# Three buffers for the tile that holds S1 and S3, and longer planned transfers, in the FFN schedule of a two-layer encoder trunk

## The chip, the cores and the metric

The kernel runs on one core of a Trainium2 chip. The metric is the device time of one execution in microseconds; a time is the median of several executions. Before the change it is 1542.79 us, the median of three runs (1539.48 to 1547.44).

## What is computed

The input is one sequence of 512 tokens of width 1024 and a memory of 256 tokens, all float32. Two layers follow one another. Each has a mixer (layer 0: forgetting and differential attention, layer 1: an mLSTM), a cross-attention to the memory, and a gated FFN with a causal convolution. Every part starts with an RMS norm and is added to the residual stream. The change touches the FFN alone:

```python
def conv_ffn(xn, w_up, conv_w, conv_b, w_down):
    h = causal_depthwise_conv(xn @ w_up, conv_w) + conv_b
    g, u = jnp.split(h, 2, axis=-1)
    return (jax.nn.gelu(g) * u) @ w_down
...
        x = x + conv_ffn(rms_norm(x, ffn_norm[layer]), ffn_w_up[layer], ffn_conv_w[layer],
                         ffn_conv_b[layer], ffn_w_down[layer])
```

`w_up` is 1024 x 5632 (2816 columns of g, 2816 of u), `w_down` is 2816 x 1024, and the convolution has three taps.

## The kernel before

**Precision.** The activations stand transposed, with the 1024 features on partitions in 8 blocks of 128 and the 512 tokens along the free dimension. Every product is done in three matmuls: each operand is split into a rounded high part (`wh`, `xh`) and the rest (`wl`, `xl`), and `mm3` (lines 268 to 270) adds high x high, high x low and low x high. A weight therefore goes through four steps before TensorE can use it: a DMA from HBM, a cast on ScalarE that makes the high part, a subtraction on VectorE that makes the low part (line 259), and the matmuls.

**Pairs.** The FFN works through 22 pairs p: block p of 128 columns of g and block p of 128 columns of u. Seven of them go through `plain`, which does the product directly. The 15 pairs in `SEVEN` (4 to 15 and 17 to 19) go through `seven`, which does the 2 x 2 block product in the seven products of Strassen's method in Winograd's form: the blocks are the two column blocks (g and u), the two halves of the 1024 features, and the two halves of 256 tokens. A1 is the weight block of g, A2 that of u, each 128 x 1024 in SBUF, whose first 512 columns belong to the first four feature blocks. The combinations of the activations (T1 to T4) are formed once in a layer by `forms` (lines 1230 to 1243, and 259), four times with k = 0 to 3, through a tile `sa` each time.

**The combinations of the weights are made by DMA.** For a pair the queue of SyncE loads, at line 1152, the first halves of A1 and A2 into a tile `sa` of 1024 columns (512 KB); GpSimd (POOL) then issues a DMA that adds A2 onto it (`b1`, line 1319). `sa` now holds S3 in its first half and S1 in its second, and `w1` splits it for p5 and p7. In the same way SyncE loads the first half of A1 into `sb` (256 KB), POOL adds the second half of `sa` onto it (`b2`: the tile is S2, split by `w2` for p6), and when that split is done, adds the second half of A1 (`b4`: the tile is S4, split by `w4` for p3). p1 and p2 take A1 itself (`raw`, split by `w3`), p4 takes the second half of A2 (`ra`, split by `w22`). The texts below write "sa load", "sa sum", "sb load", "S2 sum" and "S4 sum" for these five transfers, with the pair in brackets, s2h(5) and s2l(5) for the cast and the subtraction of `w2` of pair 5, and w1h, w1l, s4h, s4l, a22h likewise. The casts of `seven` are at line 1337, those of whole blocks at 1166.

**The products and their sums.** p1 and p2 add into one accumulator, and ScalarE writes -p1 to `v` in between (line 1373), so that p2 waits for `v`. p6, p7 and p4 add into a second one; VectorE reads it into `u2` ahead of p7 and into `u3` ahead of p4. p5 and p3 share a third one, and `c22` is read ahead of p3. `u2`, `u3`, `c22`, `c21` and `c12` are all at line 1378. There is one buffer of `v`, of `s2`, of `s4` and of `a22`. At line 1399 a pair's result is scaled; `tail` then does the convolution (ScalarE line 1257, VectorE line 1264), the gelu (1272), the product with u (1274) and the split of the result (1278 and 259).

**What fills the gaps.** From pair 5 on, `fill` puts blocks of the down projection (`down`; in the profile w<-ah,wh) between the products of a pair. Their weights come through a tile `dr` of two buffers.

**The order.** `Sched` plans every engine's order. Each piece of work is a task with an engine, a duration, the tasks it depends on, a due time and the buffers it takes and frees. A buffer is taken in the order in which the tasks were made, and a task on another engine may start `lat` after the end of what it depends on:

```python
                    for d in t.deps:
...
                        at = max(at, d.end + (0.0 if d.eng == e else d.lat))
...
                    for r, _ in t.take:
                        if want[r][0] is not t:
                            ok = False
                            break
                        at = max(at, self.slots[r][self.slot(r)])
```

At each step the task that can start first is written to the program. The framework that builds the program takes this order as a priority and sets the final order of each engine's queue by itself, so that the two differ in places. In the chip each queue then runs in order, and an instruction waits until its operands are there. The times that the plan assumes are not seen by the chip; only the order and the number of buffers are.

In the plan a load (`load`) lasts 0.0017 us a column, and a sum (`onto`) 0.0029 us a column, on their queues; what depends on them may start 2.0 and 2.5 us after that. `raw` has 3 buffers, `dr`, `sa`, `sb` and `ra` have 2 each. Buffers are used in turn.

Of the kernel before, what the change touches and what calls it, by code (L numbers as in the profile page):

```python
# [13 lines left out]
ALU = mybir.AluOpType  # L14
# [45 lines left out]
class Plan:  # L60
# [11 lines left out]
    def add(self, fn, dur=0.0, deps=(), prio=None, take=(), free=(), chain=(), pre=(), after=0.0, order=(), load=(), st=None):  # L72
        it = Item(fn, dur, [d for d in deps if d is not None], len(self.items) if prio is None else prio, take, free, chain, pre, after, order, load, st)
        it.n = len(self.items)
        self.items.append(it)
        return it
# [141 lines left out]
class Builder:  # L218
# [22 lines left out]
    def bank(self, tag):  # L241
        tag, bufs = BANKS[tag]
        return self.til(self.aux, tag, bufs=bufs)
# [875 lines left out]
    def ffn_steps(self, layer, mp):  # L1119
# [1 line left out]


        nc, t = self.nc, self.t
        sc = Sched(raw=3, h=3, s2=1, s4=1, a22=1, sa=2, sb=2, ra=2, hs=2, c=1, dr=2, v=1, u2=1, u3=1, act=10, acc=4, s=2, w=2)
        add = sc.add
        tt = lambda n: 0.14 + 1.06e-3 * n
        act = lambda n: 0.2 + 0.83e-3 * n
# [11 lines left out]
        def joined(deps, prio, free):  # L1139
            return add("-", 0.0, None, deps, prio, (), free, 0.0)  # L1140

        RAWS = {"raw": (self.wp, 1024, 3), "dr": (mp, 512, 2), "sa": (mp, 1024, 2), "sb": (mp, 512, 2), "ra": (mp, 512, 2)}

        def raw_tile(st, tag):
            pool, n, bufs = RAWS[tag]
            st[tag] = self.til(pool, tag, (P, n), bufs=bufs)
            return st[tag]

        def load(st, tag, src, cols, at):
            def fn():  # L1150
                to = raw_tile(st, tag)[:, :cols]
                nc.sync.dma_start(to.rearrange("p (a b) -> p a b", a=2) if len(src.shape) == 3 else to, src)

            return add("SP", 0.0017 * cols, fn, (), at, [(tag, st)], (), 2.0)

        def parts(st):
            st["wh"], st["wl"] = (self.til(self.wp, n, (P, 1024), F32R, bufs=3) for n in ("wh", "wl"))
# [1 line left out]
        def weight(src, cols, at, tag="raw"):  # L1159

            st = {}
            l = load(st, tag, src, cols, at - 9.0)

            def hi():
                parts(st)
                nc.scalar.copy(st["wh"][:, :cols], st[tag][:, :cols])

            h = add("ACT", act(cols), hi, [l], at - 3.0, [("h", st)])
            lo = add("DVE", tt(cols), lambda: self.sub(st["wl"][:, :cols], st[tag][:, :cols], st["wh"][:, :cols]), [h], at - 2.0, (), [(tag, st)])
            return st, lo  # L1170
# [139 lines left out]
        def seven(p, fill):  # L1310
            st, sa, sb, r2, f1, f3, s2, s4, a22 = ({} for _ in range(9))
            at = clock[0]
# [3 lines left out]


            def onto(out, src, cols, deps, due):
                return add("POOL", 0.0029 * cols, lambda: nc.gpsimd.dma_start(out(), src(), accum_op=ALU.add), deps, due, (), (), 2.5)

            SB = lambda: sb["sb"][:]
            b1 = load(sa, "sa", up2[p][:, :, :512], 1024, at - 20.0)
            b1 = onto(lambda: sa["sa"][:], lambda: A2, 1024, [b1], at - 16.0)
            b2 = load(sb, "sb", A1[:, :512], 512, at - 18.0)
            b2 = onto(SB, lambda: sa["sa"][:, 512:], 512, [b1, b2], at - 9.0)
            l2 = load(r2, "raw", A1, 1024, at - 10.0)
            l1 = load(a22, "ra", A2[:, 512:], 512, at - 6.0)
# [15 lines left out]
            w2 = split(s2, 512, [b2], at, lambda: small(s2, "s2"), [("s2", s2)], SB)  # L1343
            w1 = split(f1, 1024, [b1], at + 1.0, lambda: parts(f1), [("h", f1)], lambda: sa["sa"][:])
            b4 = onto(SB, lambda: A1[:, 512:], 512, [w2], at - 1.5)
            w22 = split(a22, 512, [l1], at + 4.0, lambda: small(a22, "a22"), [("a22", a22)], lambda: a22["ra"][:], [("ra", a22)])
            w4 = split(s4, 512, [b4], at + 5.0, lambda: small(s4, "s4"), [("s4", s4)], SB, [("sb", sb)])
# [27 lines left out]
            def sum_(tag, out, a, b, op):  # L1375
                if tag:
                    st[tag] = self.til(mp, tag, (P, 256), bufs=1)
                tt_(out=out(), in0=a(), in1=b(), op=op)
# [3 lines left out]
            hs = lambda j, l: (lambda: st["hs_"][:, j, 2 + 256 * l : 258 + 256 * l])  # L1382
            v = add("ACT", act(256), v_, [p1], at + 1.5, [("v", bv)])
            u2 = add("DVE", 0.42, lambda: sum_("u2", tmp("u2"), bank("Y"), tmp("v_"), ALU.add), [p6, v], at + 4.0, [("u2", bu2)])
# [4 lines left out]
            u3 = add("DVE", 0.42, lambda: sum_("u3", tmp("u3"), bank("Y"), tmp("v_"), ALU.add), [p7], clock[0], [("u3", bu3)])  # L1389
# [38 lines left out]
        due = {4 * c + 5 + c // 3: c for c in range(4)}  # L1428
# [384 lines left out]
```

## Time and profile before

| what | value |
|---|---|
| median of three runs | 1542.79 us (1539.48 to 1547.44) |
| the profiled execution | 1540.91 us |
| its span, first to last instruction | 1539.1 us |
| mean granted clock of TensorE | 0.990 |
| busy: TensorE, VectorE, ScalarE, POOL | 98%, 75%, 52%, 8% |
| FFN of layer 0, its Strassen pairs | about 462 to 716 us |
| FFN of layer 1, its Strassen pairs | about 1203 to 1463 us |
| DMA: from the hardware queues, from POOL's | 159.8 MB, 31.5 MB |
| share of the 16 DMA engines' span | 31.4%, 12.2% |

How rows are read. A timeline row has the start in us from the span's start, the duration, the engine, the line, the operation with out<-in, and in square brackets how long the engine was idle before it and what ended that. A row of the waits has the total, how many times, and the longest. A row of the windows has the stretch, its length, the busy time and the number of instructions (x) of TensorE's matmuls, its weight loads, VectorE, ScalarE and POOL, then the granted clock of TensorE, the mean busy share of the 16 DMA engines, and GB/s. A group row ends in busy time, mean ns of one, and idle time before it. DMA rows give the KB of one and the median us from issue to landing. In the chain of waits a row has the start, the length and what lasted that long; for a DMA that is from issue to landing. Names stand without buffer numbers; the pair of an instruction follows from its place among those of its line.

### The profile page before, as it was taken

How to read it: one execution, taken by the hardware profiler on the slowest of the kernel's cores; microseconds unless marked ns; L12 is line 12 of the kernel's file. 1: busy time of each engine (PE TensorE's matmuls, PEld its weight loads, DVE VectorE, ACT ScalarE, POOL GpSimd, SP SyncE). 2: the span in 40 equal slices, each digit the busy share in tenths (PEclk: the TensorE clock that was granted, in tenths of full speed). 3: DMA queues.
4: the chain of work that ended last, by engine and by line, in shares of the span. 5: the costliest groups of instructions: out<-in, count | busy, mean ns of one | idle time of the engine just before them, and what ended most of it. 6: DMA issues, size and time to landing. Idle time of an engine off the chain costs nothing. (4 is left out here: it accounts for less than half of the span.)

```text
span 1539.1 us, 22626 instructions
## 1 busy us (share of the span) xinstructions
PE 1501.5 (98%) x8458; PEld 1301.7 (85%) x8458; DVE 1156.7 (75%) x2167; ACT 798.6 (52%) x1342; POOL 117.3 (8%) x168
## 2 busy tenths in 40 slices
PE   9999999999998999999999999999999898989998
PEld 8888888888888988998887778888888798989987
DVE  7889875665787877888678866676658687888874
ACT  6767564443555544554446544344446454455544
POOL 2000120000001111110001000000000211111000
PEclk9999999999999999999999999999999999999999
DMA  5222232332448867752222222232324887776422
GB/s 176 83 69 83 83 125 96 110 110 69 144 143 196 207 168 196 202 149 86 86 96 82 89 77 96 96 117 76 123 83 142 187 201 188 200 172 177 114 66 76
DMA packets 72926, 193.80 MB, mean 126 GB/s; under 512 B 8048, under 2 KB 8048, under 8 KB 72816
## 3 DMA queue, kind: packets, MB, share of 16 engines
q1 hardware_dynamic: 58848, 159.77, 31.4%
q0 software_dynamic: 12960, 31.46, 12.2%
q8 instruction: 66, 1.08, 0.3%
q10 hardware_dynamic: 1008, 1.12, 0.2%
q14 instruction: 44, 0.36, 0.1%
HBM read 182.36 MB, written 2.10 MB: 120 GB/s over the span
## 5 line engine op out<-in xcount | busy, mean ns | idle before, releaser
L268 PE MATMUL acc<-xh,wh 128*128 128x512 f32 (+1 forms) x848 | 311.5, 367 | 14.9 <-ACT v L1373 14.9
L270 PE MATMUL acc<-xh,wl 128*128 128x512 f32 (+1 forms) x848 | 306.7, 362 | 0.0
L269 PE MATMUL acc<-xl,wh 128*128 128x512 f32 (+1 forms) x848 | 306.5, 361 | 0.0
L259 DVE TENSOR_TENSOR wl<-raw,wh 128x1024 fp32r<-128x1024 f32 (+2 forms) x203 | 243.6, 1200 | 42.7 <-ACT wh L262 38.1
L262 ACT CAST wh<-raw 128x1024 fp32r<-128x1024 f32 (+2 forms) x137 | 140.9, 1030 | 168.5 <-PE acc L269 99.7
L268 PEld LDWEIGHTS acc<-xh,wh 128*128 128x128 f32 x848 | 161.2, 190 | 39.4 <-ACT v L1373 16.1
L270 PEld LDWEIGHTS acc<-xh,wl 128*128 128x128 f32 x848 | 161.4, 190 | 24.1
L269 PEld LDWEIGHTS acc<-xl,wh 128*128 128x128 f32 x848 | 161.5, 190 | 23.2
L1264 DVE SCALAR_TENSOR_TENSOR c<-hs,vec,c 128x512 f32<-128x512 f32 x176 | 127.0, 747 | 11.3 <-ACT c L1257 10.7
L268 PE MATMUL w<-ah,wh 128*128 128x512 f32 x304 | 119.4, 393 | 0.0
L269 PE MATMUL w<-al,wh 128*128 128x512 f32 x304 | 119.2, 392 | 0.0
L270 PE MATMUL w<-ah,wl 128*128 128x512 f32 x304 | 118.3, 389 | 0.0
L1257 ACT ACTIVATE c<-hs,vec 128x512 f32<-128x512 f32 x88 | 69.1, 811 | 45.7 <-DVE hs L1399 39.5
L495 DVE TENSOR_TENSOR x<-w,x 128x512 f32<-128x512 f32 x72 | 49.5, 687 | 26.1 <-PE w L270 26.1
L270 PEld LDWEIGHTS w<-ah,wl 128*128 128x128 f32 x304 | 57.4, 189 | 12.3
L268 PEld LDWEIGHTS w<-ah,wh 128*128 128x128 f32 x304 | 57.6, 190 | 10.2
L269 PEld LDWEIGHTS w<-al,wh 128*128 128x128 f32 x304 | 57.6, 189 | 9.8
L330 PE MATMUL acc<-wl,xh 128*128 128x256 f32 (+1 forms) x192 | 61.9, 323 | 0.2 <-DVE wl L259 0.2
L329 PE MATMUL acc<-wh,xh 128*128 128x256 f32 (+1 forms) x192 | 61.7, 326 | 0.0
L331 PE MATMUL acc<-wh,xl 128*128 128x256 f32 (+1 forms) x192 | 61.7, 322 | 0.0
L268 PE MATMUL acc<-mem,wh 128*128 128x256 f32 (+1 forms) x192 | 61.5, 320 | 0.0
L269 PE MATMUL acc<-mem,wh 128*128 128x256 f32 (+1 forms) x192 | 61.1, 318 | 0.0
(373 smaller groups left out, 3742.1 us busy)
## 6 DMA issues: line engine op xcount, KB each, us to landing
raw<-in_up_dram SPq DMA_DIRECT2D x58, 512.0 KB, 4.5
dr<-in_down_dram SPq DMA_DIRECT2D x64, 256.0 KB, 3.3
sa<-in_up_dram SPq DMA_DIRECT2D x30, 512.0 KB, 4.7
sa<-in_up_dram POOLq DMA_DIRECT2D x30, 512.0 KB, 5.7
raw<-in_xk_dram SPq DMA_DIRECT2D x16, 512.0 KB, 3.2
raw<-in_wo_dram SPq DMA_DIRECT2D x16, 512.0 KB, 3.3
raw<-in_xq_dram SPq DMA_DIRECT2D x16, 512.0 KB, 3.2
raw<-in_xv_dram SPq DMA_DIRECT2D x16, 512.0 KB, 3.2
```

What stands on the lines that cost most here:

```text
L259: self.nc.vector.tensor_tensor(out=lo, in0=v, in1=hi.bitcast(F32), op=ALU.subtract)
L262: self.nc.scalar.copy(hi, v)
L268: mm(out, wh, xh, start=first, stop=False, skip_group_check=parts)
L269: mm(out, wh, xl, start=False, stop=False, skip_group_check=parts)
L270: mm(out, wl, xh, start=False, stop=last, skip_group_check=parts)
L329: mm(ps, xh[k][:, ts], wh[:, ws], start=(k == 0), stop=False)
L330: mm(ps, xh[k][:, ts], wl[:, ws], start=False, stop=False)
L331: mm(ps, xl[k][:, ts], wh[:, ws], start=False, stop=(k == 7))
L495: self.nc.vector.tensor_tensor(out=self.x[m][:], in0=ps[:], in1=self.x[m][:], op=ALU.add)
L1257: nc.scalar.activation(st["c_"][:, j, :], hs()[:, j, 2:514], AF.Identity, scale=self.col("cw", (layer * 3 + 2) * 44 + blk), bias=self.col( ...
L1264: nc.vector.scalar_tensor_tensor(out=c, in0=hs()[:, j, n : n + 512], scalar=w, in1=c, op0=ALU.mult, op1=ALU.add)
```

## The change

```diff
-        sc = Sched(raw=3, h=3, s2=1, s4=1, a22=1, sa=2, sb=2, ra=2, hs=2, c=1, dr=2, v=1, u2=1, u3=1, act=10, acc=4, s=2, w=2)
+        sc = Sched(raw=3, h=3, s2=1, s4=1, a22=1, sa=3, sb=2, ra=2, hs=2, c=1, dr=2, v=1, u2=1, u3=1, act=10, acc=4, s=2, w=2)
...
-        RAWS = {"raw": (self.wp, 1024, 3), "dr": (mp, 512, 2), "sa": (mp, 1024, 2), "sb": (mp, 512, 2), "ra": (mp, 512, 2)}
+        RAWS = {"raw": (self.wp, 1024, 3), "dr": (mp, 512, 2), "sa": (mp, 1024, 3), "sb": (mp, 512, 2), "ra": (mp, 512, 2)}
...
-            return add("SP", 0.0017 * cols, fn, (), at, [(tag, st)], (), 2.0)
+            return add("SP", 0.0017 * cols, fn, (), at, [(tag, st)], (), 4.0)
...
-                return add("POOL", 0.0029 * cols, lambda: nc.gpsimd.dma_start(out(), src(), accum_op=ALU.add), deps, due, (), (), 2.5)
+                return add("POOL", 0.0029 * cols, lambda: nc.gpsimd.dma_start(out(), src(), accum_op=ALU.add), deps, due, (), (), 6.0)
```

The tile `sa` gets a third buffer, in the plan and in SBUF (4 KB more on each partition). The delay that the plan adds to a load grows from 2.0 to 4.0 us, and that of a sum from 2.5 to 6.0 us. No instruction is added or removed: in the built program every engine has the same work in another order, and the waits for a slot of `sa` refer to the tile three before instead of two before. In SBUF the tiles behind `sa` move up by 4 KB.

The order moves as follows, alike in both layers. On SyncE and POOL the sa load and the sa sum of a pair stand one pair earlier among the others. On ScalarE, VectorE and TensorE the order changes around pairs 4 to 6, and in single places at pairs 9 and 10, and 13 and 14. Pieces of the built orders, before and after (cv, gelu, ah and al are steps of `tail`, dr and drl the splits of a down block, a number behind them its count):

```text
POOL    before: sa(4) S2(4) sa(5) S4(4) S2(5) sa(6) S2(6) S4(5) sa(7) S4(6) S2(7) sa(8)
        after:  sa(4) sa(5) S2(4) S2(5) sa(6) S4(4) sa(7) S4(5) sa(8) S2(6) S4(6) S2(7)
        before: S2(9) S4(8) sa(10) S2(10) S4(9) S4(10) sa(11) S2(11)
        after:  S2(9) S4(8) sa(11) S2(10) S4(9) S4(10) sa(12) S2(11)
ScalarE before: v(4) cv3 s4h(4) s2h(5) gelu3 w1h(5) c11(4) ah3 dr0 a22h(5) v(5) s4h(5) s2h(6) cv4 cv4 dr1
        after:  v(4) cv3 s4h(4) w1h(5) c11(4) gelu3 s2h(5) ah3 dr0 a22h(5) v(5) s2h(6) s4h(5) dr1
        both:   dr8 ah7 s2h(10) a22h(9) v(9) s4h(9)
VectorE before: tap3 tap3 u2(4) tap3 s4l(4) tap3 s2l(5) u(3) w1l(5) u3(4) drl0 ... c12(4) scaling(4) u2(5) s4l(5) s2l(6)
        after:  tap3 x4 w1l(5) u(3) u2(4) s2l(5) al3 s4l(4) u3(4) ... c12(4) s2l(6) scaling(4) s4l(5) u2(5)
TensorE before: p1(4) p6(4) p5(4) p2(4) p7(4) p1(5) p5(5) p4(4) p3(4) p6(5) p2(5) down p7(5)
        after:  p1(4) p5(4) p2(4) p6(4) p1(5) p7(4) p6(5) p4(4) p5(5) p3(4) p2(5) down p7(5)
        before: p1(9) p6(9) p4(8) p3(8) p5(9) p2(9)
        after:  p1(9) p6(9) p5(9) p4(8) p3(8) p2(9)
```

In the new TensorE order p2(4) stands in the middle of p5(4).

## The prediction

> **What bounds the kernel now.** I read first the page: TensorE is busy for 98% of the span, so only its idle time and a slower clock can be won back. Then the waits of TensorE, then each long one in its timeline.
>
> ```profile
> PE 1501.5 (98%) x8458; PEld 1301.7 (85%) x8458; DVE 1156.7 (75%) x2167; ACT 798.6 (52%) x1342; POOL 117.3 (8%) x168
> ...
> PE acc L268 <- ACT v L1373: 14.9, 5, 4.8
> ```
>
> ```profile
> 475.14 0.58 PE L268 MATMUL s<-th,wh 128*128 128x256 f32 x1 [4.50 <-ACT wh L1337]
> 549.20 0.58 PE L268 MATMUL acc<-xh,wh 128*128 128x256 f32 x1 [3.46 <-ACT v L1373]
> 615.01 0.39 PE L268 MATMUL acc<-xh,wh 128*128 128x256 f32 x1 [1.99 <-ACT v L1373]
> 1217.94 0.38 PE L268 MATMUL s<-th,wh 128*128 128x256 f32 x1 [4.60 <-ACT wh L1337]
> 1293.40 0.58 PE L268 MATMUL acc<-xh,wh 128*128 128x256 f32 x1 [4.79 <-ACT v L1373]
> 1361.40 0.46 PE L268 MATMUL acc<-xh,wh 128*128 128x256 f32 x1 [4.48 <-ACT v L1373]
> ```
>
> The six long waits lie in the two FFNs. Four are p2 of pairs 9 and 13 (of each layer) waiting for `v`; two are p5 of pair 5, at the start of the Strassen pairs, waiting for `w1`. The windows behind them show a second price:
>
> ```profile
> 474.10:480.90 6.80, 5.29 (x23) 5.00 (x24) 3.94 (x7) 2.30 (x5) 1.74 (x2) 0.50 0.84 178
> 549.20:552.60 3.40, 3.40 (x14) 3.30 (x15) 3.37 (x7) 2.20 (x4) 1.30 (x2) 0.50 0.62 116
> 612.80:618.00 5.20, 3.21 (x21) 2.75 (x21) 4.14 (x8) 3.12 (x6) 1.75 (x2) 1.00 0.92 217
> 1293.30:1296.70 3.40, 3.30 (x14) 3.20 (x15) 3.36 (x6) 2.04 (x5) 1.41 (x2) 0.50 0.62 106
> 1361.50:1365.00 3.50, 3.50 (x15) 3.31 (x16) 3.46 (x7) 2.14 (x4) 1.34 (x2) 0.51 0.61 118
> ```
>
> After an idle time of 3.46 us or more the granted clock is 0.50 for 3.4 us (6.8 us behind the 4.50), which loses half of it; after 1.99 us it stays 1.00.
>
> The Trainium skill ("TensorE: Matmul & The Clock Gate", Part 1) says that the clock halves after an idle window of about 3.4 us and returns after a busy one. The trace agrees: 3.46 us of idle cost 3.40 us at 0.50, and 1.99 us cost none. By that rule a wait that shrinks below some 3 us loses its second price too.
>
> **Why `v` is late: the third buffer's part.** On ScalarE's queue the cast of the S2 sum of pair 10 stands ahead of pair 9's `a22` cast and its `v`, and the built program keeps it there (s2h(10), a22h(9), v(9)) before and after the change: so the longer planned transfer doesn't reorder this. What it waits for is a sum:
>
> ```profile
> 533.10 0.33 SPq L1152 DMA_DIRECT2D sb<-in_up_dram  x1
> 534.43 0.86 POOL L1319 DMA_DIRECT2D sa<-in_up_dram  x1 [8.88 <-DVE hs L1399]
> 540.55 0.86 POOL L1319 DMA_DIRECT2D sb<-sa  x1 [5.25 <-DMA sa<-in_up_dram]
> 547.05 0.62 ACT L1337 CAST s2h<-sb 128x512 fp32r<-128x512 f32 x1 [6.97 <-DMA sb<-sa]
> 548.76 0.38 ACT L1373 ACTIVATE v<-acc 128x256 f32<-128x256 f32 x1 [0.57 <-DVE hs L1378]
> ```
>
> The S2 sum of pair 10 (540.55) waited for the sa sum of the same pair (534.43), which could not be loaded before a slot of two came free. With three slots that place in both queues belongs to pair 11, and pair 10's sa sum is done a pair earlier. Then the S2 sum waits only for its sb load and for POOL to issue pair 11's sa sum.
>
> ```profile
> sb<-in_up_dram SPq DMA_DIRECT2D x30, 256.0 KB, 4.0
> sb<-sa POOLq DMA_DIRECT2D x30, 256.0 KB, 4.3
> DMA to landing us min/median/max: 2.5/4.6/9.0
> ```
>
> Load at 533.10 + 4.0 = 537.1, issue at about 537.7; the sum takes its median 4.3 to the 6.4 of now (540.55 to the cast at 547.05): it lands at 542.0 to 544.1. From that cast to p2 it is 549.20 - 547.05 = 2.2 us, so p2 could start at 544.2 to 546.3; TensorE is ready at 549.20 - 3.46 = 545.7. Idle left: 0 to 0.6. The order of the built program also puts p5(9) ahead of p4(8) and p3(8), so `a22` and `v` of pair 9 cannot be early; I leave 0.25 a wait. The same in layer 1, where the chain of waits shows the two sums in turn:
>
> ```profile
> 1276.52 7.04 DMA sa<-in_up_dram
> ...
> 1284.39 6.77 DMA sb<-sa
> ```
>
> ```profile
> 1275.98 0.33 SPq L1152 DMA_DIRECT2D sb<-in_up_dram  x1
> ```
>
> 1275.98 + 4.0 + 0.6 = 1280.6 instead of 1284.39; landed by 1284.9 to 1287.4, p2 at 1287.1 to 1289.6, ready at 1293.40 - 4.79 = 1288.6: idle 0 to 1.0. Pair 13 has the same orders in both layers. Sum of the four: idle 3.46 + 1.99 + 4.79 + 4.48 = 14.7, half-clock losses 1.7 + 1.7 + 1.75 = 5.15, together 19.9; less 4 x 0.25 left: **-18.9 us** (bounds -20 and, where the sums gain only half of their 3 us or so, -12).
>
> **The starts: the order's part.** Here the third slot helps first: pair 4's sa load can go when the form tile before last is free, and pair 5's when pair 4's went. But the built program's queues change too. POOL: sa(4), sa(5), S2(4), S2(5), sa(6), S4(4), where it was sa(4), S2(4), sa(5), S4(4). ScalarE: s4h(4), w1h(5), c11(4), gelu, s2h(5). VectorE: w1l(5), the gelu's product, u2(4), s2l(5), al, s4l(4); before, u2(4) and s4l(4) stood ahead of all these. TensorE: p1, p5, p2, p6 of pair 4, p1(5), p7(4), p6(5), p4(4), p5(5), p3(4), p2(5).
>
> ```profile
> 454.82 1.22 DVE L259 TENSOR_TENSOR tl<-sa,th 128x1024 fp32r<-128x1024 f32 x1
> 461.53 0.86 POOL L1319 DMA_DIRECT2D sa<-in_up_dram  x1 [1.99 <-DVE c L1274]
> 463.83 0.86 POOL L1319 DMA_DIRECT2D sb<-in_up_dram  x1 [1.44 <-DVE s2l L259]
> 470.44 0.62 ACT L1337 CAST s4h<-sb 128x512 fp32r<-128x512 f32 x1 [4.47 <-DMA sb<-in_up_dram]
> 471.81 0.34 SPq L1152 DMA_DIRECT2D sb<-in_up_dram  x1
> 484.23 0.62 ACT L1337 CAST s2h<-sb 128x512 fp32r<-128x512 f32 x1 [0.97 <-DMA sb<-sa]
> 488.09 0.28 PE L268 MATMUL acc<-th,wh 128*128 128x256 f32 x1
> ```
>
> The sa load that the last form frees (454.82 + 1.22 = 456.0) was pair 5's, with its sum at 461.53; now it is pair 6's. S4(4) stands behind it: 461.53 + 0.86 = 462.4 instead of 463.83, 1.4 us earlier. It took 470.44 - 463.83 = 6.6, and has one more transfer around it: cast s4h(4) at 469 to 470.5, I take 470. Everything behind it on the two queues is worked with
>
> ```profile
> L259 DVE TENSOR_TENSOR wl<-sa,wh 128x1024 fp32r<-128x1024 f32 x15 | 18.3, 1220 | 2.2 <-ACT wh L1337 2.2
> L1274 DVE TENSOR_TENSOR c<-c 128x512 f32<-128x512 f32 x19 | 13.1, 687 | 0.6
> L1378 DVE TENSOR_TENSOR u<-acc,v 128x256 f32<-128x256 f32 x30 | 12.6, 419 | 1.2 <-PE acc L270 0.7
> L1399 DVE TENSOR_TENSOR hs<-hs,rb 128x1024 f32<-128x1024 f32 x15 | 18.3, 1221 | 0.2
> ```
>
> (the 512-wide casts 0.62, the 1024-wide one 1.05, c11 0.36, and a 512-wide subtraction like L1274's 0.69). ScalarE 0.62 + 1.05 + 0.36 + 0.62 = 2.65, then VectorE 0.69 + 0.42: u2(4) is done 3.75 us behind s4h(4), at 473.8, and p7(4) waits for it. TensorE would reach p7(4) one product (1.4 us) before it reached p5(5), 475.14 - 4.50 - 1.4 = 469.2: a wait of 4.6 us. **The stall moves from p5(5) to p7(4) and keeps its length and its half clock.** Next late is sb's slot: s4l(4) ends 2 us behind u2(4) (three times 0.69), at 475.9, and the sb load of pair 6 goes then, not at 471.81. From its issue to its cast it took 484.23 - 471.81 = 12.4; the shortest is 4.0 + 4.3 + 0.7 = 9.0. So s2h(6) at 484.9 to 488.3. VectorE has s2l(6), the scaling, s4l(5) and u2(5) in this order, 0.6 + 0.69 + 1.22 + 0.69 + 0.42 = 3.6, and p7(5) waits for u2(5): 488.5 to 491.9, middle 490.2, where it started at 488.09. TensorE itself gets there at 473.8 + 6 x 1.4 + 2.75 (one down block) + 3.4 (half clock) = 488.4, so this wait is some 1.8 us and costs no clock. **Layer 0: +2.1 (+0.4 to +3.8).**
>
> ```profile
> 1206.58 0.86 POOL L1319 DMA_DIRECT2D sb<-in_up_dram  x1 [1.63 <-DVE s2l L259]
> 1213.26 0.62 ACT L1337 CAST s4h<-sb 128x512 fp32r<-128x512 f32 x1 [4.60 <-DMA sb<-in_up_dram]
> 1214.63 0.34 SPq L1152 DMA_DIRECT2D sb<-in_up_dram  x1
> 1231.47 0.28 PE L268 MATMUL acc<-th,wh 128*128 128x256 f32 x1
> ```
>
> Layer 1 by the same steps: S4(4) up to 1.5 earlier than 1206.58, s4h(4) at 1211.8 to 1213.3, take 1212.5; s4l(4) ends at 1218.4; s2h(6) at 1227.4 to 1230.8; p7(5) at 1231.0 to 1234.4 against 1231.47. **+1.2 (-0.5 to +2.9).** The other moved instructions (sa loads and sums of pairs 7 to 19 one place earlier, w1(9) ahead of c11(8), xadd ahead of taps) find their operands ready by several us in the old trace: I cost them nothing. Their cover is the 18 us of a pair; without it, each is one more wait like those above.
>
> **Sum.** -18.9 + 2.1 + 1.2 = -15.6. The profiled execution took 1540.9 (1.8 beside its span), 1.9 below the median shown: 1525.3 there, **1527** as a median.
>
> **Rivals.** (a) The starts gain as well (0.17). S4 sums of 4.0 to 4.3 us would put s4h(4) at 466.5 and everything behind 3.5 us earlier: p7(5) 1.4 and 2.3 before its old time, so -18.9 - 3.7, 1520, or 1515 if the half-clock windows go with it. Against it: two more sa transfers run then.
> (b) The sums come as late as before (0.13). For it:
>
> ```profile
> 470.00:475.00 5.00, 0.65 (x6) 0.44 (x4) 2.65 (x4) 2.61 (x5) 1.21 (x2) 0.91 1.02 194
> ```
>
> All 16 DMA engines are full here. If pair 11's sa sum takes from S2(10) what the early issue gave, nothing is won in the middle, and the starts cost 3.3: 1546. The Trainium skill ("DMA: Bandwidth & Descriptors", Issuing engines are not separate DMA queues) speaks for it: transfers of all queues interleave on the same 16 engines. Against it: the share behind the late sums of pair 10 is 0.62.
> (c) Slower (0.12): VectorE's new order. If the S2 sum of pair 6 takes 9.0, the maximum, p7(5) is at 475.9 + 4.0 + 9.0 + 0.7 + 3.6 = 493.2, 5 us late, idle over 3.5, so 1.7 more at half clock; s4l(6), which now stands behind s2l(7), repeats it one pair later: some 13 a layer, 26 - 18.9 = +7, 1550. It decides from a loss of 9.5 us a layer.
> (d) The change does nothing because ScalarE's order at pair 9 is unchanged: it falls under (b) without its loss, 1543 (0.03).
>
> **How the numbers follow.** My forecast has 0.55: own range 1520 to 1537. With (a) below and (b) above, 8 in 10 lie in 1514 to 1546. Half a per cent, about what a measurement can tell, is 7.7 us, so faster means below 1535: 0.50 of my 0.55, all of (a) and 0.04 of the rest, 0.71; same 0.17; slower (over 1550.5) 0.12.
>
> **What would show it.** p2 of pairs 9 and 13 without idle over 1 us and with clock 1.00 behind; S2(10) issued under 5 us behind its sb load; p7(4) waiting 4 to 5 us on VectorE's `u`; the sb load of pair 6 some 4 us later against p1(4); p7(5) waiting about 2 us. Wrong if p2(9) still idles 3 us, or if TensorE waits over 3 us at a place not named here.

## The result, and the profile after

The changed kernel takes 1537.01 us (median of 15 runs, 1526.54 to 1543.52), the kernel before 1542.35 (15 runs beside them, 1537.33 to 1547.44): ratio 0.9956, 95% interval 0.9937 to 0.9975. That is a gain of 5.3 us, or 0.44%, where the prediction had 15.6. Between the two profiled executions it is 9.0 us (1540.9 and 1531.9, span 1530.1).

The page after and the waits of TensorE (line waited for, us in all, times, longest):

```profile
PE 1497.8 (98%) x8458; PEld 1299.4 (85%) x8458; DVE 1156.8 (76%) x2167; ACT 800.0 (52%) x1342; POOL 117.5 (8%) x168
```

```profile
PE acc L268 <- DVE u L1378: 12.8, 4, 3.5
PE acc L268 <- ACT v L1373: 8.2, 2, 4.2
```

There are six long waits, as before, but none is where it was. TensorE's timeline after (start, duration, what it computes, in brackets the idle time and what ended it):

```profile
469.25 0.58 PE L268 MATMUL acc<-xh,wh 128*128 128x256 f32 x1 [4.18 <-ACT v L1373]
479.45 0.58 PE L268 MATMUL acc<-th,wh 128*128 128x256 f32 x1 [3.38 <-DVE u L1378]
495.34 0.39 PE L268 MATMUL acc<-th,wh 128*128 128x256 f32 x1 [3.06 <-DVE u L1378]
554.00 0.28 PE L268 MATMUL acc<-xh,wh 128*128 128x256 f32 x1
615.15 0.28 PE L268 MATMUL acc<-xh,wh 128*128 128x256 f32 x1
1209.24 0.39 PE L268 MATMUL acc<-xh,wh 128*128 128x256 f32 x1 [4.05 <-ACT v L1373]
1219.69 0.38 PE L268 MATMUL acc<-th,wh 128*128 128x256 f32 x1 [3.51 <-DVE u L1378]
1235.52 0.38 PE L268 MATMUL acc<-th,wh 128*128 128x256 f32 x1 [2.89 <-DVE u L1378]
```

554.00 and 615.15 are p2 of pairs 9 and 13 in layer 0: no idle time. In layer 1 it is the same, since only two waits for `v` are left in the whole kernel. The rest are three waits at each start: p2(4), p7(4), p7(5). The windows behind them (stretch; busy time of PE, PEld, DVE, ACT, POOL; granted clock; DMA share; GB/s):

```profile
469.10:472.60 3.50, 3.35 (x16) 3.36 (x17) 3.35 (x5) 0.80 (x2) 0.86 (x1) 0.52 0.90 156
479.30:482.70 3.40, 3.25 (x15) 3.25 (x16) 2.18 (x5) 0.91 (x2) 1.46 (x2) 0.50 0.69 188
495.30:499.80 4.50, 4.46 (x19) 3.87 (x20) 4.50 (x9) 2.76 (x4) 0.00 (x0) 0.62 0.68 170
541.00:553.00 12.00, 12.00 (x106) 12.00 (x105) 10.10 (x16) 6.26 (x11) 2.62 (x3) 1.00 0.94 213
1209.10:1212.60 3.50, 3.36 (x17) 3.36 (x18) 3.35 (x5) 0.80 (x2) 0.00 (x0) 0.59 1.06 269
1219.60:1223.10 3.50, 3.41 (x17) 3.41 (x18) 2.48 (x6) 0.97 (x2) 1.64 (x2) 0.56 0.73 187
```

Now the account. The middle: the four waits (14.7 us idle) and their half clock (5.1) are gone, **-19.8**. The starts: before, 4.50 + 4.60 idle and two windows of 6.8 us at half clock, 15.9 in all; after, 21.1 idle (six rows) and a clock loss of 3.5 x 0.48 + 3.4 x 0.50 + 4.5 x 0.38 + 3.5 x 0.41 + 3.5 x 0.44 = 8.1, together 29.1 (behind the sixth wait the clock stays 1.00): **+13.2**. That makes -6.6 of the -9.0; the other 2.4 lie at no single row.

How a start runs now, in layer 0. POOL's queue (the sa sum of pair 5, S2(4), S2(5), S4(4)), ScalarE's casts, VectorE, and the sb load of pair 6, all from the timeline after:

```profile
454.80 0.87 POOL L1319 DMA_DIRECT2D sa<-in_up_dram  x1 [3.80 <-DVE sa L1242]
457.67 0.86 POOL L1319 DMA_DIRECT2D sb<-sa  x1 [1.99 <-DMA sa<-in_up_dram]
464.17 0.86 POOL L1319 DMA_DIRECT2D sb<-sa  x1 [5.64 <-DMA sa<-in_up_dram]
...
467.76 1.09 POOL L1319 DMA_DIRECT2D sb<-in_up_dram  x1
...
466.12 0.62 ACT L1337 CAST s2h<-sb 128x512 fp32r<-128x512 f32 x1 [6.57 <-DMA sb<-sa]
468.83 0.36 ACT L1373 ACTIVATE v<-acc 128x256 f32<-128x256 f32 x1
475.63 0.62 ACT L1337 CAST s4h<-sb 128x512 fp32r<-128x512 f32 x1 [5.74 <-DMA sb<-in_up_dram]
476.16 1.04 ACT L1337 CAST wh<-sa 128x1024 fp32r<-128x1024 f32 x1
...
477.23 1.23 DVE L259 TENSOR_TENSOR wl<-sa,wh 128x1024 fp32r<-128x1024 f32 x1 [4.78 <-ACT wh L1337]
478.98 0.42 DVE L1378 TENSOR_TENSOR u<-acc,v 128x256 f32<-128x256 f32 x1
...
481.22 0.34 SPq L1152 DMA_DIRECT2D sb<-in_up_dram  x1
...
492.53 0.69 DVE L259 TENSOR_TENSOR s2l<-sb,s2h 128x512 fp32r<-128x512 f32 x1 [3.96 <-ACT s2h L1337]
494.87 0.42 DVE L1378 TENSOR_TENSOR u<-acc,v 128x256 f32<-128x256 f32 x1
```

and of the kernel before, the sum and the cast that answer to 457.67 and 466.12:

```profile
458.67 0.87 POOL L1319 DMA_DIRECT2D sb<-sa  x1 [4.74 <-DMA sa<-in_up_dram]
...
462.19 0.62 ACT L1337 CAST s2h<-sb 128x512 fp32r<-128x512 f32 x1 [2.70 <-DMA sb<-sa]
```

The S2 sum of pair 4 went out at 457.67 (458.67 before) and its cast came 8.5 us later, not 3.5: pair 5's sa sum, issued ahead of it, ran beside it until about 464. `v` of pair 4 stands behind that cast on ScalarE, and p2(4) waits for `v`. The S4 sum of pair 4 is added into the same tile and can only go when the S2 sum is split: s2l(4) started at 466.77, the S4 sum left at 467.76 (463.83 before), and its cast came 7.9 us later. Behind it stand w1h(5), on VectorE w1l(5) and u2(4), and for u2(4) waits p7(4). The sb load of pair 6 follows at 481.22 (471.81 before); behind its sum stand s2l(6), s4l(5) and u2(5), and for this waits p7(5).

In the middle, the S2 sum of pair 10 (its sb load, its issue, its cast):

```profile
541.54 0.33 SPq L1152 DMA_DIRECT2D sb<-in_up_dram  x1
...
546.52 0.86 POOL L1319 DMA_DIRECT2D sb<-sa  x1 [3.69 <-DVE c L1264]
...
551.26 0.62 ACT L1337 CAST s2h<-sb 128x512 fp32r<-128x512 f32 x1 [2.73 <-DMA sb<-sa]
```

5.0 us from load to issue, 7.5 before (533.10 to 540.55); at the four places of the two layers it is 4.7 to 5.6, before 6.9 to 8.4. The cast comes 2.7 us ahead of p2(9) at 554.00. In the kernel before, where p2(9) waited, it was 2.2 us from one to the other (547.05 to 549.20), so the margin is some 0.6 us here, and 0 to 1.0 at the four places.

### The profile page after: what moved, and what is told of

The parts are those of the page before. It is cut to its first block, busy times and chain, and to the rows that moved or that the text cites. A ratio compares the mean times of both kernels' runs of the same rounds, so it can differ in the third digit from the quotient of the medians.

```text
span 1530.1 us, 22634 instructions
## 1 busy us (share of the span) xinstructions
PE 1497.8 (98%) x8458; PEld 1299.4 (85%) x8458; DVE 1156.8 (76%) x2167; ACT 800.0 (52%) x1342; POOL 117.5 (8%) x168
## 4 chain that ended last, share of the span: by engine, by line
PE 88%; DMA 5%; DVE 4%; ACT 2%; issue 1%; DVEq 0%; POOL 0%; POOLq 0%; ACTq 0%
PE acc L268 17%; PE acc L270 17%; PE acc L269 17%; PE w L269 5%; PE w L268 5%; PE w L270 5%; PE acc L329 3%; PE acc L331 3%; PE acc L330 3%; PE s L268 2%; PE s L270 2%; PE s L269 2%; DMA sb<-in_up_dram 2%; DMA sb<-sa 2%; DMA sa<-in_up_dram 1%
```

## The experiments

Fifteen kernels, each timed in five rounds beside the kernel before. "Profiled" is the time of the profiled execution. The medians of the kernel before differ between the groups (1540.9 us beside E1 to E4, 1543.6 beside E5 to E8, 1544.2 beside E9 to E12, 1546.8 beside E13 to E15), so kernels of different groups are compared by their ratios.

| | what it is | profiled | median | ratio to before (95%) |
|---|---|---|---|---|
| | changed kernel | 1531.9 | 1537.0 | 0.9956 (0.9937-0.9975) |
| E1 | third buffer alone | 1534.2 | 1531.7 | 0.9937 (0.9911-0.9963) |
| E2 | delays alone | 1543.9 | 1544.9 | 1.0022 (1.0002-1.0042) |
| E3 | buffer, delay of sums only | 1529.3 | 1528.9 | 0.9925 (0.9899-0.9952) |
| E4 | changed, POOL's old order at the starts | 1527.1 | 1531.8 | 0.9939 (0.9913-0.9965) |
| E5 | changed, u2(5) ahead of s2l(6) | 1541.4 | 1532.7 | 0.9913 (0.9882-0.9943) |
| E6 | E4 and E5 | 1529.8 | 1525.9 | 0.9873 (0.9844-0.9902) |
| E7 | all orders of the starts | 1524.1 | 1526.3 | 0.9882 (0.9848-0.9917) |
| E8 | the orders without POOL's | 1521.2 | 1520.2 | 0.9847 (0.9818-0.9876) |
| E9 | two buffers, v(9), v(13) first | 1535.3 | 1537.7 | 0.9957 (0.9932-0.9982) |
| E10 | E9 and orders at the starts | 1535.5 | 1537.9 | 0.9954 (0.9933-0.9976) |
| E11 | E8, u3(4) ahead of s4l(4) | 1516.3 | 1515.9 | 0.9828 (0.9785-0.9871) |
| E12 | E11 and POOL's order | 1517.7 | 1520.5 | 0.9849 (0.9811-0.9888) |
| E13 | changed, v(9), v(13) first | 1533.1 | 1531.6 | 0.9909 (0.9884-0.9933) |
| E14 | E11 and E13 | 1520.1 | 1518.5 | 0.9820 (0.9791-0.9849) |
| E15 | E9 and u2(9), u2(13) ahead of s4l | 1537.2 | 1537.3 | 0.9948 (0.9929-0.9966) |

**E1 to E3: which part of the change does what.** E1 sets the two delays back (E3 only the load's), E2 the buffer:

```diff
-            return add("SP", 0.0017 * cols, fn, (), at, [(tag, st)], (), 4.0)
+            return add("SP", 0.0017 * cols, fn, (), at, [(tag, st)], (), 2.0)
...
-                return add("POOL", 0.0029 * cols, lambda: nc.gpsimd.dma_start(out(), src(), accum_op=ALU.add), deps, due, (), (), 6.0)
+                return add("POOL", 0.0029 * cols, lambda: nc.gpsimd.dma_start(out(), src(), accum_op=ALU.add), deps, due, (), (), 2.5)
```

> The third buffer with the old planned delays (2.0 us for a load, 2.5 us for a sum). Theory: the buffer alone brings the gain in the middle: p2 of pairs 9 and 13 waits less than 1 us in both layers (3.5, 2.0, 4.8 and 4.5 us before, none in the changed kernel). POOL has the order of the changed kernel at the starts (the sa sum of pair 5 ahead of pair 4's S2 sum, that of pair 6 ahead of pair 4's S4 sum), so p2 of pair 4 waits 4 us there too, and the profiled execution takes 1529 to 1535 us. Rival: the gain comes from the longer planned delays; then the four waits stay at 2 to 5 us each and the time is that of before, 1539 to 1546 us or more.

TensorE's long waits in layer 0 of E1:

```profile
482.25 0.58 PE L268 MATMUL acc<-th,a22h 128*128 128x256 f32 x1 [8.46 <-DVE u L1378]
555.77 0.58 PE L268 MATMUL acc<-xh,wh 128*128 128x256 f32 x1 [4.67 <-ACT v L1373]
```

Three of the four waits in the middle are gone without the delays; p2(9) of layer 0 still waited 4.67 us here. The start came out otherwise than expected: no wait of p2(4), but one of 8.5 us at p4(4), whose u3 stands behind w1l(5) and s4l(4) on VectorE. So the profiled time lies in the theory's range by other waits than the theory's.

> Two buffers, as before, with the new planned delays (4.0 us for a load, 6.0 us for a sum). Theory: the delays bring no gain in the middle (four waits of p2 of pairs 9 and 13, 12 to 18 us together with their half clock), and POOL keeps its order of before at the starts, so that p2 of pair 4 does not wait; time 1537 to 1546 us. Rival: the delays bring the gain; then the four waits are below 1 us each and the time is 1525 to 1533 us.

```profile
PE acc L268 <- ACT v L1373: 15.8, 8, 4.4
```

Of these, 10.2 us are the four places of the middle (14.7 before), with 6.8 us of half clock: they stay, and the delays alone win nothing and may lose 0.2%. But p2(4) waited too (1.5 and 2.9 us), which the theory had not. Its S2 sum took 3.5 and 3.3 us here, as before; what is new is TensorE's order, which has p2(4) ahead of p6(4) and of most of p5(4).

> Three buffers, the planned load at its old 2.0 us, the planned sum at the new 6.0 us. TensorE's order at the starts differs from that of the changed kernel (p5 of pair 4 whole ahead of p6, p1 and p2 of pair 5 where the changed kernel has p6 of pair 5), POOL's is the same up to pair 5. Theory: the waits at the starts come from the order of the sums on POOL; then p2 of pair 4 waits 3.5 to 5 us here too, the starts cost within 3 us a layer of those of the changed kernel, and the time is within 4 us of it. Rival: they come from TensorE's or ScalarE's order; then the three waits of a layer (11 us idle) fall to one, and the time is 1520 to 1526 us.

The profiled time is the theory's, the place is not: p2(4) did not wait, p7(4) waited 1.9 us and p4(4) 4.0 and 3.6; p2(13) of layer 0 waited 3.1. So the stall of a start takes another place with each order, and is 5.5 to 11 us idle a layer in E1, E3 and the changed kernel.

**E4: POOL's order.** The sa sums of pairs 5 and 6 go behind pair 4's S2 and S4 sums again:

```diff
-            b1 = onto(lambda: sa["sa"][:], lambda: A2, 1024, [b1], at - 16.0)
+            b1 = onto(lambda: sa["sa"][:], lambda: A2, 1024, [b1] + (acts["s3"] if p in (5, 6) else []), at - 16.0)
...
-            b2 = onto(SB, lambda: sa["sa"][:, 512:], 512, [b1, b2], at - 9.0)
+            b2 = onto(SB, lambda: sa["sa"][:, 512:], 512, [b1, b2], at - 9.0); acts["s3"] = [b2]
```

(and the sa sums of pairs 5 and 6 keep their planned place in POOL's queue).

> The changed kernel with one thing undone: at the starts POOL issues as before, pair 4's S2 sum ahead of pair 5's sa sum and pair 4's S4 sum ahead of pair 6's sa sum; all other engines keep the order of the changed kernel but for one cast. Theory: the sa sums put ahead made pair 4's sums late (8.4 and 7.8 us from issue to landing in layer 0, against 3.5 and 6.6 before). Then pair 4's S2 sum takes 3.5 to 5 us again, p2 of pair 4 waits below 1 us, and the time is 1520 to 1527 us. Rival: all 16 DMA engines are full there, so that the order only moves the wait to p7 of pairs 4 and 5; then the idle time of a start stays at 10 to 12 us a layer and the time within 3 us of the changed kernel's.

S2(4), S4(4) and their casts in E4, and the waits of layer 0:

```profile
457.54 0.87 POOL L1319 DMA_DIRECT2D sb<-sa  x1 [6.95 <-DMA sa<-in_up_dram]
465.49 0.86 POOL L1319 DMA_DIRECT2D sb<-in_up_dram  x1 [6.19 <-DVE s2l L259]
...
463.85 0.62 ACT L1337 CAST s2h<-sb 128x512 fp32r<-128x512 f32 x1 [4.46 <-DMA sb<-sa]
470.03 0.62 ACT L1337 CAST s4h<-sb 128x512 fp32r<-128x512 f32 x1 [2.40 <-DMA sb<-in_up_dram]
...
466.98 0.39 PE L268 MATMUL acc<-xh,wh 128*128 128x256 f32 x1 [2.07 <-ACT v L1373]
473.85 0.39 PE L268 MATMUL acc<-th,wh 128*128 128x256 f32 x1 [1.47 <-DVE u L1378]
491.64 0.58 PE L268 MATMUL acc<-th,wh 128*128 128x256 f32 x1 [5.76 <-DVE u L1378]
```

S4(4) took 4.5 us (7.9 in the changed kernel), S2(4) still 6.3, with pair 5's sa sum now right behind it. The waits of p2(4) and p7(4) fell by half and p7(5)'s grew from 3.1 to 5.8: 9.3 us idle in a layer instead of 10.6. By these rows POOL's order is a part of the cause, the smaller one; the ratios of E4 and of the changed kernel do not tell the two apart.

**E5 to E8: ready work behind work that waits.** These kernels add orders to the queues; a rule (a, b) means that a stands behind b on their engine, in the plan (as a dependency of its task) and in the built program (the other instructions are marked as `v` is here):

```diff
+        tasks, RULES, marks = {}, [(("s2l", 6), ("u2", 5)), ], {}
+        order = lambda a, b: self.tc.add_manual_dep(marks[a].ins, marks[b].ins.name, mybir.DependencyInfo(mybir.DependencyClass.NoSync, mybir.DependencyReason.DATA), reason="order")
+        mark = lambda k, i: (marks.update({k: i}), [order(a, b) for a, b in RULES if k in (a, b) and a in marks and b in marks])
...
-                nc.scalar.activation(st["v_"][:], st["X"][:, :256], AF.Copy, scale=-1.0)
+                mark(("v", p), nc.scalar.activation(st["v_"][:], st["X"][:, :256], AF.Copy, scale=-1.0))
```

E5 has this rule alone. E6 adds (sa sum 5, S2 4) and (sa sum 6, S4 4); E7 adds to these (s2h 4, v 4), (s4h 4, w1h 5), (w1l 5, u2 4), (S2 5, S4 4) and (sa sum 7, sa sum 6). E8 has (s2l 6, u2 5), (s2h 4, v 4) and (sa sum 7, S4 4), so that POOL's order at the start is the changed kernel's up to S2(6).

> The changed kernel with one added order: VectorE computes pair 5's u2 ahead of the low part of pair 6's S2 (s2l). Theory: p7 of pair 5 waits 3.1 to 3.2 us in each layer only because u2 stands in VectorE's queue behind s2l, which waits for the S2 sum of pair 6. Then that wait falls below 1 us and no other takes its place (p6 of pair 6, which needs the same sum, comes 12 us later); p2 and p7 of pair 4 still wait 4.2 and 3.6 us; the profiled execution takes 1521 to 1526 us, against 1531.9. Rival: the sum of pair 6 itself is what TensorE waits for; then the wait moves to p6 of pair 6 and the time stays within 3 us of 1531.9.

Both readings were wrong: p7(5) still waited 3.7 us in layer 0 (1.1 in layer 1), p7(4) of layer 1 rose to 5.9, and in this execution two waits of the middle were back (p2(13) 3.1, p2(9) of layer 1 4.2), which is why it took 1541.4; the median is 1532.7.

> The order of sums on POOL of the run before (pair 4's S2 and S4 sums ahead of the sa sums of pairs 5 and 6) together with pair 5's u2 ahead of pair 6's s2l on VectorE. There p7 of pair 5 waited 5.9 and 5.7 us and lost half a clock window behind it. Theory: both go, since the S2 sum of pair 6 was on time for its own product; the profiled execution takes 1510 to 1516 us against 1527.1 of the run before. Rival: the DMA engines are what is late, and the wait moves on to p6 of pair 6 or p3 of pair 5; then 1523 to 1529 us.

p7(5) of layer 0 waited 5.8 us again, and p2(13) 3.4. The rule had moved one instruction only; ScalarE and VectorE of E6 ahead of that product:

```profile
489.39 0.62 ACT L1337 CAST s2h<-sb 128x512 fp32r<-128x512 f32 x1 [9.52 <-DMA sb<-sa]
489.92 0.61 ACT L1337 CAST s4h<-sb 128x512 fp32r<-128x512 f32 x1
...
490.56 0.69 DVE L259 TENSOR_TENSOR s4l<-sb,s4h 128x512 fp32r<-128x512 f32 x1 [7.14 <-ACT s4h L1337]
491.17 0.42 DVE L1378 TENSOR_TENSOR u<-acc,v 128x256 f32<-128x256 f32 x1
```

u2(5) no longer stands behind s2l(6), but behind s4l(5), whose cast stands on ScalarE behind s2h(6): the same late sum, by way of another engine. The S4 sum of pair 5 had left at 476.0 and, with no transfer of `sb` there over 6.4 us, had landed by 482.4: its cast was ready 7 us before it ran. The Trainium skill (PSUM — Partial Sum Buffer, Engine vs sequencer instructions) calls the queues of ScalarE, VectorE and GpSimd strict FIFO; these four rows agree.

> All orders at the start set by hand: on POOL pair 4's S2 and S4 sums ahead of the sa sums of pairs 5 and 6; on ScalarE v of pair 4 ahead of the cast of its S2 sum and the cast of pair 5's w1 ahead of that of pair 4's S4 sum; on VectorE u2 of pair 4 ahead of pair 5's w1 low part and u2 of pair 5 ahead of pair 6's s2l. Theory: the waits of the starts come from queues in which ready work stands behind work that waits for a sum. Then no wait over 2 us is left in either FFN, and the time is 1506 to 1514 us. Rival: the sums of pairs 4 and 5 cannot come earlier, and p6 or p3 of these pairs wait for them instead, 8 us or more a layer; time 1520 to 1530 us.

1524.1: no wait at p2(4), p7(4) and p7(5), but p4(5) waited 5.4 and 5.8 us for its u3, which stood behind s2l(6). TensorE's order is another one here too: p5(5) and a down block stand on either side of p4(4).

> The changed kernel, its sums on POOL in their own order (pair 5's sa sum still ahead of pair 4's S2 sum), with v of pair 4 ahead of the cast of its S2 sum on ScalarE (which also brings the cast of pair 5's w1 ahead of that of pair 4's S4 sum) and u2 of pair 5 ahead of pair 6's s2l on VectorE. Theory: the sums stay late (S2 of pair 4 landing 3 us after p1 of pair 4 starts, S4 12 us after it) but little stands behind them; p6 and p3 of pair 4 wait up to 2 us each, 2 to 5 us a layer in all, against 11; time 1513 to 1520 us. Rival: POOL's order is the whole cause; the waits go to p6 and p3 of pair 4 with 8 us or more a layer, time 1525 to 1532 us.

1521.2, near the theory's range, with POOL as in the changed kernel. One long wait is left in a start, at p4(4) (5.3 and 5.4 us; p7(5) 1.4 and 1.6), and not where the theory had it. VectorE of E8 ahead of it:

```profile
477.41 0.69 DVE L259 TENSOR_TENSOR s4l<-sb,s4h 128x512 fp32r<-128x512 f32 x1 [6.06 <-ACT s4h L1337]
478.02 0.42 DVE L1378 TENSOR_TENSOR u<-acc,v 128x256 f32<-128x256 f32 x1
```

u3(4) stands behind s4l(4). So with the sums as late as in the changed kernel (S4(4) left at 466.98 and was cast at 476.76) and the same order on TensorE, the order on ScalarE and VectorE alone wins 10.7 us of its profiled execution (1531.9 to 1521.2); its medians' ratio interval lies wholly below that of the changed kernel.

**E9, E10, E15: is the third buffer needed?** E9 is the kernel of before with the rules (s2h 10, v 9), (s2l 10, u2 9) and the same for 14 and 13; E10 adds (s4h 4, w1h 5), (s2h 5, w1h 5), (w1l 5, u2 4), (s4l 4, u3 4), (s2l 6, u2 5), (s2h 6, s4h 5); E15 is E9 with (s4l 9, u2 9), (s4l 13, u2 13).

> The kernel of before, with two buffers and the old delays, and one added order at pairs 9 and 13: on ScalarE v goes ahead of the cast of the next pair's S2 sum, on VectorE u2 goes ahead of that sum's low part. Theory: the four waits of before were a queue order (ready casts behind a cast that waits for a sum), so that they go without any third buffer; the waits and their half clock were 19.9 us, 0 to 1 us a place is left, the profiled execution takes 1521 to 1526 us against 1540.9. Rival: the sum is truly late without a third buffer, and p7 of pairs 9 and 13 or p6 of pairs 10 and 14 wait for it instead; then 1535 to 1543 us.

p2(9) and p2(13) wait no more, but p7 of these pairs does, 1.9 to 3.2 us in all four places, for a u2 that stands behind s4l(9) or s4l(13).

> The run before, plus orders at the starts with two buffers: the cast of pair 5's w1 ahead of those of pair 4's S4 sum and pair 5's S2 sum, u3 of pair 4 ahead of its s4l, the cast of pair 5's S4 sum and u2 of pair 5 ahead of pair 6's S2 sum. Theory: p5 of pair 5 (4.5 and 4.6 us idle and a half clock behind it before) then waits 0 to 2 us, and p6 of pair 5 up to 2 us for its S2 sum; 1510 to 1519 us. Rival: the wait of the start is that of the DMA engines and moves to p3 of pair 4 or p6 of pair 5 whole; then the time is that of the run before within 3 us.

p5(5) lost its wait as the theory has it; p4(5) took its place (5.4 us at the longest), and the time is E9's.

> Two buffers and the old delays, v of pairs 9 and 13 first as in the run of this kind before, where p7 of these pairs still waited 2.0 to 3.4 us for u2; now u2 goes ahead of s4l too. Theory: the third buffer is not needed for the middle: p2 and p7 of pairs 9 and 13 wait below 1 us, the profiled execution takes 1523 to 1530 us and the median lies at 0.985 to 0.991 of the kernel of before. Rival: with two buffers the sums themselves are too late, and p4 or p3 of pairs 9 and 13 or p6 of pairs 10 and 14 wait in p7's place; 1533 to 1539 us, 0.994 to 0.998.

TensorE and ScalarE of E15 behind v(9):

```profile
552.86 0.50 PE L268 MATMUL w<-ah,wh 128*128 128x512 f32 x1 [1.15 <-ACT wh L1166]
...
550.25 0.62 ACT L1337 CAST s4h<-sb 128x512 fp32r<-128x512 f32 x1 [4.17 <-DMA sb<-in_up_dram]
550.78 1.52 ACT L1257 ACTIVATE c<-hs,vec 128x512 f32<-128x512 f32 x2
552.20 0.60 ACT L1166 CAST wh<-dr 128x512 fp32r<-128x512 f32 x1
```

With p7 free, a down block waits for a cast that stands behind s4h(9), and that for its sum: 1.2 to 2.2 us in four places. Three orders with two buffers give 0.9948 to 0.9957 each; in none did all four places run free, as they did with three. Whether more rules would get there was not tried.

**E11, E12, E14: the fastest.** E11 is E8 with (s4l 4, u3 4); E12 adds (sa sum 5, S2 4), (sa sum 6, S4 4) and (sa sum 7, sa sum 6) in place of (sa sum 7, S4 4).

> The run with three buffers and orders without POOL's, and u3 of pair 4 ahead of pair 4's s4l on VectorE. There p4 of pair 4 waited 5.4 and 5.6 us for u3, which stood behind s4l, and that for the S4 sum. Theory: p4 goes at once and only p3 of pair 4 waits, 1 to 2.5 us, no half clock; the profiled execution takes 1508 to 1515 us against 1521.2. Rival: the sum decides, and p3 of pair 4 waits 5 us in p4's place; then 1517 to 1523 us.

1516.3, between the two: p4(4) goes at once and p3(4) waits 2.7 and 3.4 us.

> As the run before, with POOL's order at the starts that of the kernel of before as far as the S2 and S4 sums of pair 4 go ahead of the sa sums of pairs 5 and 6. Theory: with the queue orders mended, the sa sum of pair 5 issued early (as the changed kernel does) is no loss; put behind pair 4's S2 sum it makes pair 5's S2 sum late by 5 us or so, and p6 of pair 5 waits 2 to 5 us; time 2 to 10 us above the run before. Rival: POOL's order is what cost the changed kernel its gain; then this one is 2 to 6 us faster than the run before.

The median is 4.5 us above E11's, but the intervals overlap: not told apart. p6(5) did not wait, as the theory had it; what waited were down blocks and p7(4), 1.1 to 1.9 us each. A gain from POOL's old order no longer shows once the queues are mended.

**E13 and E14: what the median has above the profile.** The rules of E9 and E15 for pairs 9 and 13, and (sa sum 12, S4 10), on the changed kernel and on E11.

> The changed kernel with one added order at pairs 9 and 13: v ahead of the cast of the next pair's S2 sum on ScalarE, u2 ahead of s4l and of the next pair's s2l on VectorE; its starts are left as they are. Theory: the median of the changed kernel (1537.0) lies 5.1 us above its profiled execution because p2 of pairs 9 and 13 still waits in some executions when that sum is late (in the profiles of the kernels with this order so far, 5 of 24 such places waited 3.2 to 4.8 us). With v ahead none waits; the median is 1529 to 1534 us and the profiled execution 1528 to 1533. Rival: what the median has above that execution lies in the three waits of each start; then the median stays at 1535 to 1539 us.

1531.6, six executions from 1529.0 to 1535.5 (fifteen from 1526.5 to 1543.5 in the changed kernel), with the starts still waiting 3.1 to 5.2 us. ScalarE of E13 at pair 9:

```profile
550.47 0.39 ACT L1373 ACTIVATE v<-acc 128x256 f32<-128x256 f32 x1
551.84 0.62 ACT L1337 CAST s2h<-sb 128x512 fp32r<-128x512 f32 x1 [0.99 <-DMA sb<-sa]
```

p2(9) started at 551.16 without a wait. Behind that cast, as in the changed kernel, it would have come 2.2 us after 551.84 at the earliest, 2.9 us late. The theory's number came out. But the starts were not quite the same: in E13's profiled execution they had two waits a layer (p2(4), p7(4)) and cost 26.3 us with the clock, 29.1 in the changed kernel, so that a part of the lower median may lie there. That the longer executions of the changed kernel are late sums of the middle is inferred from E13 and from the waits counted in other kernels: none of them was profiled.

> The same order at pairs 9 and 13 added to the three-buffer kernel with u3 first (the fastest so far, median 1515.9, executions from 1512.3 to 1528.5). Theory: the slow ones of its executions are late S2 sums of pairs 10 and 14, so that the median falls to 1509 to 1515 us and the highest execution to 1521 or less. Rival: its middle was already clear, and the spread lies in the starts; median 1514 to 1519 us with the same spread.

1518.5, four executions within 4 us of each other (E11: six within 16), ratio 0.9820 against 0.9828: the same time, above what the theory had. The longest execution (1520.1) is what it had, but four are few to judge a spread by.

## Why the prediction was wrong in size

The median came out 10 us above the forecast (1537.0 for 1527). Of these, 6.6 lie in the profiled execution (1531.9 for 1525.3): the starts cost 9.9 more than forecast, the middle won 0.9 more, and 2.4 were won at no single row. The rest is that the median lies 5.1 us above the profiled execution, where the prediction took over the 1.9 of the kernel before.

- **The four waits of the middle, -18.9.** Right: -19.8 by the rows of the profiled execution, for the reason given (the S2 sum leaves 4.7 to 5.6 us behind its sb load; E1 shows that the buffer does it, E2 that the delays don't). But 0.25 us was left a wait as if every execution were alike. The margin is 0 to 1.0 us, and transfers vary by more: in the changed kernel, E1 and E3 to E6, which have this order of `v` and s2h, the wait was there at 5 of 24 places; in E8, E11, E12 and at pair 13 of E7, which have it too, at none of 14. At four places an execution, 5 in 24 or 5 in 38, and 3.7 us a wait with 1.7 us of half clock, that is an estimated 2.8 to 4.5 us of the 5.1.
- **The starts, +2.1 and +1.2.** This is the step that failed: they cost +13.2. It had one wait a layer move from p5(5) to p7(4) and keep its length. That one came (3.4 and 3.5 us for the 4.6 forecast, with a half clock half as long), but two more came with it. First, p2(4) was not looked at: the text read that POOL issues pair 5's sa sum ahead of S2(4), and gave S2(4) no price for it. S2(4) took 8.5 us, not 3.5 (in layer 1 5.8, not 3.3), and `v`(4) stands behind its cast (4.2 and 4.1 us). The late sum needs TensorE's new order beside it: in E1, with sums of 7.2 and 7.5 us and p6(4) and p5(4) still ahead of p2(4), p2(4) did not wait, and in E2 the new order alone made it wait 1.5 and 2.9 us. Second, the prediction had S4(4) leave at 462.4, by POOL's queue alone. It waits for s2l(4), as the prediction's own row at 463.83 says (1.44 idle, ended by s2l), and so it followed the late S2(4): it left at 467.76. Its 7.9 us to the cast are near the 7.6 allowed for. So the cast came at 475.6 instead of 470, and the sb load of pair 6 left at 481.2, not at 475.9; p7(5) waited 3.1 and 2.9 us and not 1.8, and in layer 0 lost clock.
- **"What would show it"**: p2(9) and p2(13) clear with clock 1.00 came out. S2(10) left 4.98 us behind its load in layer 0, just under the 5 named, and 5.59 in layer 1. p7(4) waited on `u`, but under the 4 to 5 us named, and p7(5) over the 2. "Wrong if TensorE waits over 3 us at a place not named" came out too: p2(4).
- **Rivals.** (a) had the starts gain by S4 sums of 4.0 to 4.3 us; S4(4) took 7.9 and they lost. (b) had the DMA engines full at the starts and in this was right (share 0.90 and 1.06 behind p2(4)), but nothing was lost in the middle. (c) had VectorE's order as what loses: its place was one of the three (s2l(6) and s4l(5) ahead of u2(5)), its size was 13 us a layer where 6.6 came for all three. The result is the forecast's middle with half of (c)'s loss at the starts.
- The other moved instructions cost nothing that a wait shows.

## What to carry to other kernels

When a list of transfers is issued earlier, price each accumulating DMA that then runs beside them, and follow each late one through every in-order queue to the product behind it: here one late sum held up ready casts on ScalarE, through them VectorE, and through it TensorE. With the third buffer there, setting the order in those queues was worth more (ratio 0.9956 to 0.9828) than the change itself; without it, the three sets of orders tried gave 0.9948 to 0.9957. A rule that moves one instruction only moves the wait, as long as other ready work still stands behind the late cast. A margin shorter than the spread of a transfer can show as a wait in some executions and not in others, so one profile can put a gain too high (the changed kernel's lay 5.1 us below its median) or too low (E5's lay 8.7 us above).

## What was not expected of the hardware

The clock halved after shorter idle times than the 3.46 us of before. In the changed kernel 3.06 us was enough (0.62 in the window at 495.30) and 2.89 was not (the wait that ends at 1235.52), but in E6 2.52 us was (the wait that ends at 1209.65).

So the length of the wait alone does not decide; the Trainium skill ("TensorE: Matmul & The Clock Gate", Part 1) has about 3.4 us, and here the measurement decides. What else does is in the traces. In each trace the falls of the clock lie whole multiples of 3.41 us apart (in the changed kernel they come at 469.07, 479.31, 496.37, 1209.76 and 1220.00), so the time can be cut into stretches of 3.41 us that end where the clock may change. The stretches with most of these three waits, of the changed kernel and, last, of E6:

```profile
492.96:496.37 3.41, 1.03 (x8) 1.03 (x9) 3.41 (x6) 2.76 (x6) 0.86 (x1) 1.00 0.37 59
1233.65:1237.07 3.42, 1.55 (x13) 1.55 (x14) 3.42 (x6) 2.36 (x5) 0.86 (x1) 1.00 0.54 81
...
1206.13:1209.54 3.41, 1.00 (x9) 0.79 (x7) 2.36 (x4) 3.02 (x6) 0.86 (x1) 1.00 0.80 211
```

TensorE is busy for 1.03, 1.55 and 1.00 of 3.41 us, and in the next stretch the clock is 0.50, 1.00 and 0.50. Over the 17 traces, from 40 to 1500 us, a stretch at full clock with 1.94 us idle or more was always followed by one at half clock, one with less than 1.66 never, and between the two both occur. A stretch at half clock was followed by another where 0.61 us or more of it was idle, and by full clock where it was 0.43 or less. So a wait of 1.89 us, all in one stretch, lost clock in E9 (p7(13) of layer 0; 0.50 from 616.64 on), and one of 2.43 us across two stretches lost none in E14 (p3(4) of layer 0). The prediction's reading that a wait below some 3 us costs no clock does not hold here.
